# A hybrid encoder layer on one core: rotary tables moved behind the recurrence's convolutions, gate weights cleared and loaded earlier, softplus in a tile of its own

## The chip, the core and the metric

The kernel is one program on one core of a Trainium2 chip. A core has a matrix engine (PE, with its weight loads shown apart as PEld), a vector engine (DVE), an activation engine (ACT), a general engine (POOL) and a queue engine (SP) that issues DMA transfers. Each engine runs its own list of instructions in order; semaphores tie the lists together. Working tiles lie in on-chip memory (128 partitions wide), and PE writes its products into PSUM, from which DVE and ACT read.

The metric is the device time of one execution in microseconds (us), as the median of several runs. The profile is of one further execution and shows every instruction of every engine.

## The reference

One layer of a bidirectional encoder for 1024 tokens of width 1024 in f32. The part that matters here is the first of its three sub-layers, up to the attention:

```python
h = rms_norm(x, attn_norm)
proj = h @ w_in                       # 512 xr | 512 y | 256 q-latent | 128 kv-latent | 32 rope key
xf = depthwise_conv(xr, lru_conv_w[0], lru_conv_b[0], 3, 0)      # causal, width 4
xb = depthwise_conv(xr, lru_conv_w[1], lru_conv_b[1], 0, 3)      # anti-causal
hf = rg_lru(xf, w_a[0], b_a[0], w_i[0], b_i[0], lam[0], False)
hb = rg_lru(xb, w_a[1], b_a[1], w_i[1], b_i[1], lam[1], True)
lru_out = (hf + hb) * gelu(yg)

def rg_lru(x, w_a, b_a, w_i, b_i, lam, reverse):
    r = sigmoid(block_diag(x, w_a) + b_a)
    i = sigmoid(block_diag(x, w_i) + b_i)
    log_a = -8.0 * r * softplus(-lam)
    b = sqrt(-expm1(2.0 * log_a)) * (i * x)
    # h[t] = exp(log_a[t]) * h[t-1] + b[t], or from the right if reverse

def rope_tables(positions):
    inv = 10000.0 ** (-arange(0, 32, 2) / 32)
    ang = positions[..., None] * inv
    return cos(ang), sin(ang)
...
```

The tables rotate the last 32 columns of each query head and the shared rope key in the attention. Behind the attention come a cross-attention to a memory of 256 tokens and a gated feed-forward part with a width-3 convolution, which take most of the time and are not touched.

## The kernel before

The input is normalised in eight tiles of 128 tokens and transposed by PE into `hT` (L189 to L201), split into a rounded part and a remainder. Every product is made of three (`mm3`, L109): rounded by rounded, rounded by remainder, remainder by rounded. The weights are split in the same way, POOL doing the two steps (`wsplit`, L134 and L135) for all but the first.

The recurrent branch works in four units of 128 channels. For unit j, `xr_stage(j)` makes the projection (PSUM tile `psin`, two of these in turn) and both convolutions of width 4: ACT writes bias plus first tap for each direction (L348), then DVE adds three taps per direction, reading `psin` each time (L350 forward, L352 backward). `y_stage(j)` makes the gate branch's projection in the other `psin` and the gelu on ACT and DVE (L359 Square, L360, L361 Tanh, L362). `lru_stage(j)` makes for each direction the two gates (four products `psg`, L381), then the decay (Exp, L384), the input factor (Tanh L385, Sqrt L386, L388), the gated input (L389, L390 on POOL) and the scan on DVE (L393 forward, L395 backward); L397 and L399 join the directions with the gelu. A new projection can start only when the `psin` tile of the projection two before has been read for the last time: by the sixth convolution step of an `xr` unit (L352), or by the gelu's last step of a `y` unit (L362).

The stages are written in this order: xr 0, xr 1, gate weights 0, rotary tables, y 0, lru 0, xr 2, y 1, gate weights 1, lru 1, xr 3, y 2, lru 2, y 3, lru 3, then the latents (`lat_units`, `latents`, L403 on, PSUM tile `pslat` from the same pair as `psin`) and the attention. The code order is not the order on the engines: a scheduler places the instructions on each engine's list by its own estimates, and only the dependences and `tc.issue_after` bind it.

`rope_tables()` (L442) computes the sine and cosine arguments of 8 x 16 x 128 angles in a tile `rtt`: 16 one-column memsets on POOL (L445), 45 DVE instructions on 128x128 elements (L448 to L499, argument reduction in several parts), two Sin on ACT (L480, L481) and two small DMA loads of the gains (L483, L484). `rtt` has the tag "yt" with one buffer, which is also the tag of the gelu's tile `t` in `y_stage`: the tiles of the two follow one another in program order. `krs`, `rS`, `rqC` and `rqS` are its results; the first to be read is `krs`, by POOL's rotation of the shared key after the latents (`rotated`, L438 to L441).

`gate_unit(jj)` (L315) takes a tile `wgate`, clears it on POOL (L318), and loads the diagonal blocks with eight DMAs (L323).

The 15 parameter rows are loaded into the first 128 columns of a tile `RR` of six times 128 columns (L203, tag "xr", two buffers), transposed by PE and copied to `pcols`, which every bias and tap reads. The softplus of the recurrence's decay is computed from `pcols` on POOL with two steps on DVE (L277 to L296), with its temporaries `e8`, `y8`, `z8`, `w8` in `RR[:, 5]`. The convolution tiles of xr 1 have the tag "xr" as well, so that one of them has to wait until `RR` is read for the last time.

Of the kernel before, what the change touches and what calls it, by code (L numbers as in the profile page):

```python
# [11 lines left out]
F32 = mybir.dt.float32  # L12
# [3 lines left out]
ALU = mybir.AluOpType  # L16
# [3 lines left out]
S = 1024  # L20
# [63 lines left out]
def trunk_layer(ctx: ExitStack, tc: tile.TileContext, a: dict, out: bass.AP):  # L84
# [91 lines left out]
            w_first = wsplit(w_in_load(0), eng="ad")  # L176
    w_second = w_in_load(P)


    hT = [[big.tile([P, KD, 512], F32R, tag="big", name=f"hT{h}{s}") for s in range(2)] for h in range(2)]  # L180
    scr = lrup.tile([P, NJ, S], F32, tag="lru", name="scr")
# [19 lines left out]
            last_lo = dve.tensor_sub(hT[h][1][:, q * 4:q * 4 + 4, o:o + P], pv, f(hT[h][0])[:, q * 4:q * 4 + 4, o:o + P])  # L201


    RR = tp.tile([P, 6, P], F32, tag="xr", bufs=2, name="RR")
    R1, R2, R3 = RR[:, 0], RR[:, 1], RR[:, 2]
    pool.memset(R1, 0.0)
    rows = {}
# [2 lines left out]
    def addrows(name, ap, n, w=P):  # L210
        r = pos[0]
        rows[name] = r
        pos[0] += n
        nc.sync.dma_start(R1[r:r + n, :w], ap)
# [13 lines left out]
    addrows("mk_g", a["mem_k_norm"], 1)  # L228
    addrows("q_g", a["mla_q_norm"], 1, QKH)
    addrows("k_g", a["mla_k_norm"], 1, QKH)  # L230
    pcols = const.tile([P, P], F32, name="pcols")
    pt = pb1.tile([P, 512], F32, tag="b1", name="ptp")
    pe.transpose(pt[:, :P], R1, ident)
# [36 lines left out]
    pool.tensor_scalar(hb, cols("b_a", 16), 0.5, 0.0, ALU.mult, ALU.add)  # L270
    sp4 = const.tile([P, 16], F32, name="sp4")
    lam = cols("lam", 8)
    e8 = RR[:, 5, 0:8]
    y8 = RR[:, 5, 8:16]
    z8 = RR[:, 5, 16:24]
    w8 = RR[:, 5, 24:32]
    pool.tensor_scalar(z8, lam, -1.0, 0.0, ALU.mult, ALU.add)  # L277
    dve.tensor_tensor(z8, z8, lam, ALU.min)
    pool.memset(e8, math.e)
# [30 lines left out]
        return ps  # L310

    lru = lrup.tile([P, NJ, S], F32, tag="lru", name="lru")
    wg = {}

    def gate_unit(jj):  # L315

        w = wp.tile([P, 1024], F32, tag="w", name="wgate")
        pool.memset(w, 0.0)  # L318
        rv = w.rearrange("p (j d g c) -> p j d g c", j=2, d=2, g=2)
        for b in range(2):  # L320
            for gi, nm in enumerate(("lru_w_a", "lru_w_i")):
                for d in range(2):
                    nc.sync.dma_start(  # L323
                        rv[64 * b:64 * b + 64, :, d, gi, 64 * b:64 * b + 64],
                        a[nm][0, d].rearrange("(j b) p c -> b p j c", b=2)[b][:, 2 * jj:2 * jj + 2, :])
        wg[jj] = w

    ssl = const.tile([P, NT], F32, name="ssl")
    ssm = const.tile([P, NT], F32, name="ssm")
    krss = bc.tile([P, NT], F32, name="krss")  # L330
# [11 lines left out]
    def xr_stage(j):  # L342

        ps = in_proj(j * P)
        xfs = [tp.tile([P, S], F32, tag=("xf", "xr")[j % 2], bufs=2, name="xf") for _ in range(2)]
        cw = [[col("conv_w", (d * 4 + k) * 4 + j) for k in range(4)] for d in range(2)]
        for d in range(2):
            act.activation(xfs[d], ps, AF.Identity, bias=col("conv_b", d * 4 + j), scale=cw[d][3 - 3 * d])  # L348
        for n in range(1, 4):
            dve.scalar_tensor_tensor(xfs[0][:, n:], ps[:, :S - n], cw[0][3 - n], xfs[0][:, n:], ALU.mult, ALU.add)  # L350
        for n in range(1, 4):
            dve.scalar_tensor_tensor(xfs[1][:, :S - n], ps[:, n:], cw[1][n], xfs[1][:, :S - n], ALU.mult, ALU.add)  # L352
        return xfs

    def y_stage(j):
# [48 lines left out]
    def lat_units():  # L404
        for kk in range(4):
            def load(raw, kk=kk):
                nc.sync.dma_start(raw[:, :2 * LAT].rearrange("p (k c) -> p k c", k=2),
                                  w_in[kk * 2 * P:(kk + 1) * 2 * P, OFF_CQ:OFF_CQ + LAT].rearrange("(k p) c -> p k c", p=P))
            wl_.append(wunit(load, 2 * LAT))
# [31 lines left out]
    def rope_tables():  # L441
# [59 lines left out]
            rS.append(T)  # L501
        return rC, rS

    xrs = {0: xr_stage(0)}
    xrs[1] = xr_stage(1)
    gate_unit(0)
    rC, rS = rope_tables()
    y_stage(0)
    lru_stage(0, xrs[0])
    xrs[2] = xr_stage(2)  # L510
    y_stage(1)
    gate_unit(1)
    lru_stage(1, xrs[1])
    xrs[3] = xr_stage(3)
# [1 line left out]
    lru_stage(2, xrs[2])  # L516
    y_stage(3)
    lru_stage(3, xrs[3])
    lat_units()
    for t in range(NT):  # L520
        latents(t)
# [746 lines left out]
```

## Time and profile before

| | us |
|---|---|
| median of three runs | 1434.71 |
| the three runs | 1434.5, 1434.71, 1444.2 |
| the profiled execution, own time | 1439.12 |
| its span in the profile | 1437.0 |

The profiled execution lasted 2.1 us longer than the span that its profile shows, and 4.4 us longer than the median. A row of the timeline gives start, duration, engine, line, operation, output and inputs, the shapes, a count, and in brackets how long the engine had been idle before it and what released it. A row with a count above 1 puts neighbouring instructions of one form together, with the sum of their time. A row of the windows view gives, for a stretch of time, its length and the busy time of each engine (with the count of instructions), then the clock granted to PE (1.00 is full), the share of the DMA engines and the rate.

### The profile page before, as it was taken

How to read it: one execution, taken by the hardware profiler on the slowest of the kernel's cores; microseconds unless marked ns; L12 is line 12 of the kernel's file. 1: busy time of each engine (PE TensorE's matmuls, PEld its weight loads, DVE VectorE, ACT ScalarE, POOL GpSimd, SP SyncE). 2: the span in 40 equal slices, each digit the busy share in tenths (PEclk: the TensorE clock that was granted, in tenths of full speed). 3: DMA queues.
4: the chain of work that ended last, by engine and by line, in shares of the span. 5: the costliest groups of instructions: out<-in, count | busy, mean ns of one | idle time of the engine just before them, and what ended most of it. 6: DMA issues, size and time to landing. Idle time of an engine off the chain costs nothing.

```text
span 1437.0 us, 18317 instructions
## 1 busy us (share of the span) xinstructions
PE 1377.6 (96%) x6832; PEld 1153.7 (80%) x6832; DVE 903.6 (63%) x1236; ACT 603.0 (42%) x955; POOL 579.3 (40%) x597
## 2 busy tenths in 40 slices
PE   6898899998999999999999999999999999999998
PEld 5666698787889888888887888888888888888887
DVE  6787747899998856576644665443443445665553
ACT  5374945688888842355422111111111122433331
POOL 6653544557696811021239999322332310000000
PEclk9899999999999999999999999999999999999999
DMA  5301101200000052101008888322223222666763
GB/s 197 84 14 42 61 16 45 74 1 1 1 1 1 14 170 81 46 14 30 30 17 285 288 292 275 125 80 89 96 92 99 96 74 96 198 213 206 222 195 103
DMA packets 114231, 145.94 MB, mean 102 GB/s; under 512 B 9546, under 2 KB 64095, under 8 KB 114143
## 3 DMA queue, kind: packets, MB, share of 16 engines
q1 hardware_dynamic: 114143, 144.78, 31.0%
q8 instruction: 54, 0.88, 0.3%
q14 instruction: 34, 0.28, 0.1%
HBM read 105.95 MB, written 38.80 MB: 101 GB/s over the span
## 4 chain that ended last, share of the span: by engine, by line
PE 77%; DVE 9%; ACT 7%; POOL 2%; issue 2%; DMA 1%; SPq 0%; ACTq 0%; DVEq 0%; POOLq 0%
PE psup L109 33%; PE psdn L109 8%; PE psdw L109 6%; PE psP L109 6%; PE psq L109 3%; PE psS L109 3%; PE psmo L109 3%; PE po L109 3%; PE psin L109 2%; PE pslat L109 2%; PE psT L767 2%; DVE st L748 2%; DVE pT L771 2%; PE pq L109 1%; PE pkv L109 1%
## 5 line engine op out<-in xcount | busy, mean ns | idle before, releaser
L109 PE MATMUL psup<-h,whi 128*128 128x512 f32 x1408 | 434.4, 389 | 1.1 <-DVE gu L1158 0.9
L109 PEld LDWEIGHTS psup<-h,whi 128*128 128x128 f32 x1408 | 264.2, 188 | 56.6 <-POOL ws L1182 1.2
L109 PE MATMUL psup<-h,wlo 128*128 128x512 f32 x704 | 273.9, 389 | 0.0
L1157 DVE SCALAR_TENSOR_TENSOR gu<-psup,fcw,gu 128x1023 f32<-128x1023 f32 x44 | 56.4, 1281 | 187.6 <-ACT gu L1156 183.0
L1156 ACT ACTIVATE gu<-psup,fcw 128x1024 f32<-128x1024 f32 x44 | 53.3, 1211 | 287.2 <-PE psup L109 287.2
L1215 DVE TENSOR_TENSOR dlo<-rawd,dhi 128x1024 fp32r<-128x1024 f32 x77 | 93.5, 1223 | 101.0 <-ACT dhi L1214 101.0
L109 PEld LDWEIGHTS psup<-h,wlo 128*128 128x128 f32 x704 | 132.2, 188 | 27.4
L1214 ACT ACTIVATE dhi<-rawd 128x1024 fp32r<-128x1024 f32 x77 | 81.5, 1061 | 158.7 <-PE psdn L109 51.0
L134 POOL TENSOR_SCALAR whi<-raw 128x1024 fp32r<-128x1024 f32 (+2 forms) x58 | 70.2, 1210 | 192.0 <-PE psup L109 176.6
L135 POOL TENSOR_TENSOR wlo<-raw,whi 128x1024 fp32r<-128x1024 f32 (+2 forms) x58 | 143.8, 2479 | 9.1 <-PE psin L109 5.7
L109 PE MATMUL psS<-kT,qT 96*128 96x512 f32 x384 | 103.8, 404 | 3.9 <-ACT pr L752 3.8
L109 PE MATMUL psin<-hT,whi 128*128 128x512 f32 (+1 forms) x288 | 88.2, 390 | 7.9 <-DVE xf L352 6.6
L754 POOL TENSOR_SCALAR pr<-pr,st 128x1024 f32<-128x1024 f32 x64 | 72.0, 1125 | 54.1 <-DVE st L753 32.2
L771 DVE TENSOR_TENSOR pT<-psT,pT 128x512 fp32r<-128x512 f32 x128 | 84.4, 678 | 5.9 <-ACT pT L770 5.8
L752 ACT ACTIVATE pr<-psS,st,rqk 128x1024 f32<-128x1024 f32 x64 | 77.2, 1207 | 17.8 <-DVE st L750 13.3
L748 DVE TENSOR_REDUCE st<-psS 128x1 f32<-128x1024 f32 x64 | 77.7, 1214 | 8.1 <-PE psS L109 7.8
L109 PEld LDWEIGHTS psS<-kT,qT 96*128 96x128 f32 x384 | 67.6, 189 | 17.6 <-ACT pr L752 6.2
L1182 POOL TENSOR_TENSOR ws<-rawd 128x512 f32<-128x512 f32 x55 | 81.4, 1508 | 0.0
L109 PE MATMUL po<-pT,vt 128*128 128x256 f32 x512 | 72.3, 287 | 3.9 <-DVE pT L771 3.7
L770 ACT ACTIVATE pT<-psT 128x512 fp32r<-128x512 f32 x128 | 70.9, 596 | 8.1 <-PE psT L767 7.6
L767 PE MATMUL psT<-ident,pr 128*128 128x128 f32 x512 | 68.3, 273 | 5.7 <-POOL pr L754 3.7
L109 PEld LDWEIGHTS psin<-hT,whi 128*128 128x128 f32 x288 | 54.7, 198 | 21.1 <-issue 9.6
(303 smaller groups left out, 2832.5 us busy)
## 6 DMA issues: line engine op xcount, KB each, us to landing
raw<-in_w_up SPq DMA_DIRECT2D x44, 512.0 KB
rawd<-ad SPq DMA_DIRECT2D x77, 256.0 KB
wd<-ws SPq DMA_DIRECT2D x55, 256.0 KB
ad<-as SPq DMA_DIRECT2D x55, 256.0 KB
rawd<-wd SPq DMA_DIRECT2D x55, 256.0 KB
rawd<-in_w_down SPq DMA_DIRECT2D x22, 512.0 KB
ad<-gu SPq DMA_DIRECT2D x22, 256.0 KB
rawd<-in_w_down SPq DMA_DIRECT2D x22, 256.0 KB
```

The lines of the kernel that those rows point to most:

```text
L109: return pe.matmul(ps, lhsT=l, rhs=r, start=start, stop=stop)
L134: pool.tensor_scalar(hi[:, sl], raw[:, sl], 1.0, 0.0, ALU.mult, ALU.add)
L135: pool.tensor_sub(lo[:, sl], raw[:, sl], f(hi)[:, sl])
L748: dve.tensor_reduce(st[:, 0:1], psS, AX.X, ALU.max, negate=True)
L752: act.activation(pr, psS, AF.Exp, bias=st[:, 1:2], scale=r, accum_out=st[:, 2:3])
L754: scaled[s] = pool.tensor_scalar(pr, pr, st[:, 3:4], 0.0, ALU.mult, ALU.add)
L767: pe.transpose(ps[:, i * P:(i + 1) * P], pr[:, (n * 4 + i) * P:(n * 4 + i + 1) * P], ident)
L770: act.activation(dh, pv, AF.Copy)
L771: dve.tensor_sub(pTs[s // 2][n][1][:, :, qi * P:(qi + 1) * P], pv, f(dh))
L1182: pool.tensor_tensor(st, raws[h0][:, c0], raws[h1][:, c1], op)
L1214: act.activation(hi, raw, AF.Copy)
L1215: dve.tensor_sub(lo, raw, f(hi))
```

## The change

Three things change in the source.

The call of `rope_tables()` goes from between `xr_stage(1)` and `y_stage(0)` to behind `lru_stage(3)`, with the condition that none of its instructions is issued ahead of the last backward convolution step of the last unit (`last_conv[-1]`). Since `rtt` shares the buffer "yt", its 16 memsets now wait for the gelu of `y_stage(3)`.

`gate_unit` is split: `gate_zero(jj)` clears the tile, `gate_unit(jj)` loads it. For the first two units of the recurrence the clearing is placed ahead of the input's normalisation, and the loading right behind the parameter rows. For the other two both stand where `gate_unit(1)` stood.

`RR` loses its sixth row, and softplus's temporaries get a small tile `spc` of their own, so that softplus no longer keeps a convolution tile of xr 1 waiting.

```diff
+    def gate_zero(jj):
+        wg[jj] = wp.tile([P, 1024], F32, tag="w", name="wgate")
+        pool.memset(wg[jj], 0.0)
+    def gate_unit(jj):
+        rv = wg[jj].rearrange("p (j d g c) -> p j d g c", j=2, d=2, g=2)
...
+    gate_zero(0)
...
-    RR = tp.tile([P, 6, P], F32, tag="xr", bufs=2, name="RR")
+    RR = tp.tile([P, 5, P], F32, tag="xr", bufs=2, name="RR")
...
     addrows("k_g", a["mla_k_norm"], 1, QKH)
+    gate_unit(0)
...
-    e8 = RR[:, 5, 0:8]
-    y8 = RR[:, 5, 8:16]
-    z8 = RR[:, 5, 16:24]
-    w8 = RR[:, 5, 24:32]
+    spc = sm.tile([P, 4, 8], F32, tag="spc", bufs=1, name="spc")
+    e8, y8, z8, w8 = spc[:, 0], spc[:, 1], spc[:, 2], spc[:, 3]
...
-            dve.scalar_tensor_tensor(xfs[1][:, :S - n], ps[:, n:], cw[1][n], xfs[1][:, :S - n], ALU.mult, ALU.add)
+            last_conv.append(dve.scalar_tensor_tensor(xfs[1][:, :S - n], ps[:, n:], cw[1][n], xfs[1][:, :S - n],
+                                                      ALU.mult, ALU.add))
...
+    last_conv = []
     xrs = {0: xr_stage(0)}
     xrs[1] = xr_stage(1)
-    gate_unit(0)
-    rC, rS = rope_tables()
     y_stage(0)
     lru_stage(0, xrs[0])
     xrs[2] = xr_stage(2)
     y_stage(1)
+    gate_zero(1)
     gate_unit(1)
...
     lru_stage(3, xrs[3])
+    with tc.issue_after(last_conv[-1].ins):
+        rC, rS = rope_tables()
     lat_units()
```

The scheduler makes another order of this on every engine up to the attention; behind that the orders are the same. Most line numbers of the kernel after are larger by 2 to 5 from `gate_unit`'s old place on (convolution L352 and L354, gelu L362 to L365, recurrence L384 to L402, tables L451 to L502), and by 17 or 18 ahead of it.

On DVE, this is what stood around the first convolutions before (the numbers in the names tell buffers apart; `xf_463` and `xf_464` are the two directions of unit 0):

```order
L282 RECIPROCAL RR_285<-RR_285 128x8
L459 SCALAR_TENSOR_TENSOR rtt_546<-rtt_546 128x128
L350 SCALAR_TENSOR_TENSOR xf_463<-psin_366,pcols_302,xf_463 128x1023
L459 SCALAR_TENSOR_TENSOR rtt_546<-rtt_546 128x128
L350 SCALAR_TENSOR_TENSOR xf_463<-psin_366,pcols_302,xf_463 128x1022
L453 TENSOR_SCALAR rtt_546<-rtt_546 128x128
L470 TENSOR_TENSOR rtt_546<-rtt_546 128x128
L350 SCALAR_TENSOR_TENSOR xf_463<-psin_366,pcols_302,xf_463 128x1021
L352 SCALAR_TENSOR_TENSOR xf_464<-psin_366,pcols_302,xf_464 128x1023
```

And this is DVE's list at the same place in the kernel after (`xf_474` and `xf_475` are unit 0, `xf_537` the forward direction of unit 1):

```order
L295 TENSOR_TENSOR spc_337<-spc_337,pcols_312 128x8
L352 SCALAR_TENSOR_TENSOR xf_474<-psin_377,pcols_312,xf_474 128x1023
L352 SCALAR_TENSOR_TENSOR xf_474<-psin_377,pcols_312,xf_474 128x1022
L352 SCALAR_TENSOR_TENSOR xf_474<-psin_377,pcols_312,xf_474 128x1021
L354 SCALAR_TENSOR_TENSOR xf_475<-psin_377,pcols_312,xf_475 128x1023
L299 RECIPROCAL spc_337<-spc_337 128x8
L354 SCALAR_TENSOR_TENSOR xf_475<-psin_377,pcols_312,xf_475 128x1022
L352 SCALAR_TENSOR_TENSOR xf_537<-psin_488,pcols_312,xf_537 128x1023
L354 SCALAR_TENSOR_TENSOR xf_475<-psin_377,pcols_312,xf_475 128x1021
```

The table steps are gone from here, softplus's reciprocal stands between two steps of the backward convolution, and one step of unit 1 stands ahead of unit 0's sixth.

In the middle of the recurrence the convolutions of unit 3 stood on DVE as follows before (`xf_955` is unit 3's forward direction, `thi_863` and `thi_885` the two directions of unit 1, whose forward scan L393 stood ahead of all convolutions of unit 2):

```order
L360 SCALAR_TENSOR_TENSOR yt_839<-yt_839,psin_790 128x1024
L362 SCALAR_TENSOR_TENSOR lru_358<-yt_839,psin_790 128x1024
L389 SCALAR_TENSOR_TENSOR thi_885<-thi_885,xf_527 128x1024
L388 SCALAR_TENSOR_TENSOR thr_884<-av_890,thr_884 128x1024
L395 SCALAR_TENSOR_TENSOR thi_885<-av_890,thi_885 128x1024
L397 TENSOR_TENSOR thi_863<-thi_863,thi_885 128x1024
L399 SCALAR_TENSOR_TENSOR lru_358<-thi_863,lru_358 128x1024
L350 SCALAR_TENSOR_TENSOR xf_955<-psin_906,pcols_302,xf_955 128x1023
```

The same stretch of DVE's list after (`xf_889` is unit 3's forward direction, `thi_797` and `thi_819` the two directions of unit 1):

```order
L363 SCALAR_TENSOR_TENSOR yt_773<-yt_773,psin_724 128x1024
L365 SCALAR_TENSOR_TENSOR lru_369<-yt_773,psin_724 128x1024
L392 SCALAR_TENSOR_TENSOR thi_797<-thi_797,xf_537 128x1024
L391 SCALAR_TENSOR_TENSOR thr_796<-av_802,thr_796 128x1024
L396 SCALAR_TENSOR_TENSOR thi_797<-av_802,thi_797 128x1024
L392 SCALAR_TENSOR_TENSOR thi_819<-thi_819,xf_538 128x1024
L391 SCALAR_TENSOR_TENSOR thr_818<-av_824,thr_818 128x1024
L398 SCALAR_TENSOR_TENSOR thi_819<-av_824,thi_819 128x1024
L352 SCALAR_TENSOR_TENSOR xf_889<-psin_840,pcols_312,xf_889 128x1023
L400 TENSOR_TENSOR thi_797<-thi_797,thi_819 128x1024
L352 SCALAR_TENSOR_TENSOR xf_889<-psin_840,pcols_312,xf_889 128x1022
```

Both directions of unit 1 now stand between the gelu of `y_stage(1)` and unit 3's convolutions, and the joins L400 and L402 stand between the convolution's steps.

At the end of the recurrence, where before only the steps of unit 3 stood (L397 and L399 of unit 2, then L388, L390 and L393 of unit 3), DVE's list after reads (`thi_1074` is unit 3's forward direction):

```order
L365 SCALAR_TENSOR_TENSOR lru_369<-yt_1060,psin_1011 128x1024
L400 TENSOR_TENSOR thi_968<-thi_968,thi_990 128x1024
L392 SCALAR_TENSOR_TENSOR thi_1074<-thi_1074,xf_889 128x1024
L451 TENSOR_TENSOR rtt_1111<-posc_332,rtt_1111 128x128
L402 SCALAR_TENSOR_TENSOR lru_369<-thi_968,lru_369 128x1024
L456 TENSOR_SCALAR rtt_1111<-rtt_1111 128x128
L457 TENSOR_SCALAR rtt_1111<-rtt_1111 128x128
L391 SCALAR_TENSOR_TENSOR thr_1073<-av_1079,thr_1073 128x1024
L466 SCALAR_TENSOR_TENSOR rtt_1111<-rtt_1111 128x128
L456 TENSOR_SCALAR rtt_1111<-rtt_1111 128x128
L393 TENSOR_TENSOR thi_1074<-thi_1074,thr_1073 128x1024
```

Five of the 45 table steps (L451, L456, L457, L466, L456) now stand ahead of unit 3's product L393; the others follow it, among the scans and the latents' scalings.

On SP's queue these loads stood behind the parameter rows before (rows of the same form are counted):

```order
L214 DMA RR<-in_mla_k_norm 1x96
L249 DMA RR<-in_ffn_conv_w 88x128
L250 DMA RR<-in_ffn_conv_w 44x128
L251 DMA RR<-in_ffn_conv_b 44x128
L260 DMA RR<-in_positions 8x128
L483 DMA rtt<-in_mla_q_norm 128x32
L484 DMA rtt<-in_mla_k_norm 128x32
L155 DMA raw<-in_w_in 128x8x128 x2
L323 DMA wgate<-in_lru_w_a 64x2x64 x2
L323 DMA wgate<-in_lru_w_i 64x2x64 x2
```

After, the same place of SP's queue has:

```order
L232 DMA RR<-in_mla_k_norm 1x96
L191 DMA wgate<-in_lru_w_a 64x2x64 x2
L191 DMA wgate<-in_lru_w_i 64x2x64 x2
L191 DMA wgate<-in_lru_w_a 64x2x64 x2
L191 DMA wgate<-in_lru_w_i 64x2x64 x2
L268 DMA RR<-in_ffn_conv_w 88x128
L269 DMA RR<-in_ffn_conv_w 44x128
L270 DMA RR<-in_ffn_conv_b 44x128
L279 DMA RR<-in_positions 8x128
L155 DMA raw<-in_w_in 128x8x128 x5
```

The eight gate loads come ahead of the third input weight block and of the positions, and the two gain loads of `rtt` have left; they stand now behind the load of `w_ukv` and ahead of those of `w_mem_kv`.

More of the change, by code (lines that the diff above doesn't have):

```diff
@@ L177, in trunk_layer @@
     w_second = w_in_load(P)
+    wg = {}
+    def gate_zero(jj):
[3 more added lines that the diff above has]
+        rv = wg[jj].rearrange("p (j d g c) -> p j d g c", j=2, d=2, g=2)
+        for b in range(2):
+            for gi, nm in enumerate(("lru_w_a", "lru_w_i")):
+                for d in range(2):
+                    nc.sync.dma_start(
+                        rv[64 * b:64 * b + 64, :, d, gi, 64 * b:64 * b + 64],
+                        a[nm][0, d].rearrange("(j b) p c -> b p j c", b=2)[b][:, 2 * jj:2 * jj + 2, :])
+    gate_zero(0)
     hT = [[big.tile([P, KD, 512], F32R, tag="big", name=f"hT{h}{s}") for s in range(2)] for h in range(2)]
@@ L312, in trunk_layer @@
     lru = lrup.tile([P, NJ, S], F32, tag="lru", name="lru")
[L313 to L326, printed above, removed]
     ssl = const.tile([P, NT], F32, name="ssl")
```

## The prediction

> **What bounds the kernel now.** I read the busy shares first, then PE's idle stretches up to the attention in the windows view, then the timeline of the engine that ends each of them.
>
> ```profile
> PE 1377.6 (96%) x6832; PEld 1153.7 (80%) x6832; DVE 903.6 (63%) x1236; ACT 603.0 (42%) x955; POOL 579.3 (40%) x597
> core 0: us, PE busy (x) PEld busy (x) DVE busy (x) ACT busy (x) POOL busy (x), PEclk, DMA share, GB/s
> 33.90:38.40 4.50, 4.50 (x17) 3.72 (x18) 3.05 (x5) 1.08 (x2) 4.33 (x4) 0.62 0.55 147
> 50.50:56.70 6.20, 0.08 (x1) 0.00 (x0) 6.20 (x10) 1.20 (x1) 5.70 (x9) 0.90 0.48 124
> 56.70:62.60 5.90, 5.86 (x8) 2.53 (x9) 4.37 (x7) 1.73 (x3) 4.53 (x17) 0.52 0.56 158
> 109.80:115.00 5.20, 0.09 (x1) 0.00 (x0) 5.10 (x5) 0.30 (x1) 1.11 (x2) 0.86 0.28 82
> 115.00:120.00 5.00, 4.92 (x12) 3.89 (x13) 3.44 (x3) 3.87 (x5) 0.00 (x0) 0.50 0.00 0
> 139.60:173.30 33.70, 33.70 (x128) 23.70 (x126) 23.32 (x17) 33.39 (x37) 16.34 (x10) 1.00 0.19 59
> 185.00:211.00 26.00, 26.00 (x146) 25.47 (x145) 8.20 (x15) 8.43 (x29) 7.50 (x12) 1.00 0.00 1
> 42.60:71.50 28.90, 16.14 (x45) 0.62 (x2) 0.00 (x0) 0.88 0.28 75
> ```
>
> The last row counts the tile `rtt` alone; its engines are DVE, ACT and POOL. PE works 96% of the span, so the whole gain lies in a few waits. DVE is busy in all of 50.5 to 56.7 and nearly all of 109.8 to 115.0 while PE stands still, and PE runs at half clock behind each. From 139.6 to 173.3 ACT is busy for 33.39 of 33.70 us: there ACT is the bound, and PE's time means little. From 185 on PE is never idle, so what arrives there is carried to the end.
>
> **First gate and first gelu projection.** These rows end PE's first wait:
>
> ```profile
> 44.93 2.31 ACT L348 ACTIVATE xf<-psin,pcols 128x1024 f32<-128x1024 f32 x2 [9.29 <-DVE rtt L459]
> 46.37 2.45 POOL L135 TENSOR_TENSOR wlo<-raw,whi 128x1024 fp32r<-128x1024 f32 x1
> 46.61 3.20 DVE L454 TENSOR_SCALAR rtt<-rtt 128x128 f32<-128x128 f32 x1
> 50.20 0.39 PE L109 MATMUL psin<-hT,wlo 128*128 128x512 f32 x1
> 50.80 0.19 DVE L282 RECIPROCAL RR<-RR 128x8 f32<-128x8 f32 x1
> 55.26 1.27 DVE L350 SCALAR_TENSOR_TENSOR xf<-psin,pcols,xf 128x1021 f32<-128x1021 f32 x1
> 56.74 6.44 PE L109 MATMUL psg<-xf,wgate 128*128 128x512 f32 x8 [6.16 <-issue]
> 59.31 1.27 DVE L352 SCALAR_TENSOR_TENSOR xf<-psin,pcols,xf 128x1021 f32<-128x1021 f32 x1
> 62.62 1.02 PE L109 MATMUL psin<-hT,whi 128*128 128x512 f32 x2
> 62.84 0.20 POOL L296 TENSOR_SCALAR sp<-sp 128x8 f32<-128x8 f32 x1
> 73.94 3.59 PE L109 MATMUL psg<-xf,wgate 128*128 128x512 f32 x8
> ```
>
> The gate at 56.74 starts right behind the third forward step (55.26 + 1.27 = 56.53). The forward direction's bias was there at 44.93 + 1.16 = 46.1, so without the table steps its three convolution steps (1.27 each) end at 49.9. PE finishes the second projection at 50.20 + 0.39 = 50.6. The gate then follows at 50.6, 6.1 earlier, without the idle time. The y 0 projection needs the sixth step: by the new order seven convolution steps and a reciprocal stand ahead on DVE, 46.1 + 7 x 1.27 + 0.2 = 55.2, against 62.62: -7.4. PE is free from 54.2 by the warm gate duration (3.59 instead of 6.44 for 8 rows), so PE waits only about 1 us there.
>
> **To the end of y 1.**
>
> ```profile
> 70.97 1.24 ACT L384 ACTIVATE av<-thr,sp 128x1024 f32<-128x1024 f32 x1
> 75.95 2.58 DVE L388 SCALAR_TENSOR_TENSOR thr<-av,thr 128x1024 f32<-128x1024 f32 x1 [0.79 <-ACT thr L386]
> 84.43 0.70 PE L109 MATMUL psin<-hT,whi 128*128 128x512 f32 x2 [1.42 <-DVE xf L352]
> 106.50 1.02 ACT L359 ACTIVATE yt<-psin 128x1024 f32<-128x1024 f32 x1 [8.57 <-PE psin L109]
> ```
>
> A projection takes 73.94 - 62.62 = 11.3, or (106.50 - 84.43) / 2 = 11.0. Between y 0 and xr 2 PE had two sets of gates and 1.4 + 1.4 us of waits; now one set stands there, the second goes behind y 1. So 55.2 + 11.3 + 3.6 + 22.1 = 92.2, against 106.50: -14.3. Softplus was ready at 62.84 + 0.20 = 63.0 and no table step delays it now; with the Exp not ahead of 63.0 and 75.95 - 70.97 = 5.0 from Exp to Sqrt, ACT is through at 68, behind which y 0's Square comes. That is 1.4 after y 0's end (66.5), hidden under the gates and xr 2.
>
> **Unit 3's projection and y 2.**
>
> ```profile
> 88.05 1.23 DVE L388 SCALAR_TENSOR_TENSOR thr<-av,thr 128x1024 f32<-128x1024 f32 x1 [0.46 <-ACT thr L386]
> 89.36 2.40 POOL L390 TENSOR_TENSOR thi<-thi,thr 128x1024 f32<-128x1024 f32 x1 [8.38 <-DVE thr L388]
> 98.29 3.24 DVE L397 TENSOR_TENSOR thi<-thi 128x1024 f32<-128x1024 f32 x1
> 115.08 1.19 PE L109 MATMUL psin<-hT,whi 128*128 128x512 f32 x2 [5.19 <-DVE xf L352]
> 126.85 2.29 DVE L395 TENSOR_TENSOR_SCAN thi<-av,thi 128x1024 f32<-128x1024 f32 x1 [2.51 <-POOL thi L390]
> 139.60 1.02 ACT L359 ACTIVATE yt<-psin 128x1024 f32<-128x1024 f32 x1 [8.58 <-PE psin L109]
> 149.03 1.06 ACT L386 ACTIVATE thr<-thr 128x1024 f32<-128x1024 f32 x1
> ```
>
> Unit 3's projection waits for unit 2's sixth convolution step, which stands behind both directions of unit 0 and their joins. From y 0's Square at 68 to the next Sqrt's end ACT takes 149.03 + 1.06 - 139.60 = 10.5: 78.5. Then L388 1.23, the product 2.40 and the scan 2.29 give 84.4; the two joins 1.2 to 3.2 each and six steps 7.6 give 94.4 to 98.4. I take 96.4, the middle, since PE is free at 95.8 anyway (92.2 + 3.6): -18.7 against 115.08. From there to y 2's end it was 139.60 - 115.08 = 24.5. The half-clock stretch (4.92 us of work at 0.50, 2.5 us lost) does not come without a wait of PE, and one set of gates more lies inside: 24.5 - 2.5 + 3.6 = 25.6, so 122.0: -17.6.
>
> **y 3, where a new wait opens.** Now both directions of unit 1 stand on DVE ahead of unit 3's convolutions, and y 3 needs the sixth of these.
>
> ```profile
> 142.43 1.03 PE L109 MATMUL psin<-hT,whi 128*128 128x512 f32 x2
> 157.54 1.06 ACT L386 ACTIVATE thr<-thr 128x1024 f32<-128x1024 f32 x1
> 158.50 1.01 ACT L359 ACTIVATE yt<-psin 128x1024 f32<-128x1024 f32 x1
> 179.12 0.71 PE L109 MATMUL pslat<-whi,hT 128*128 128x416 f32 x1 [5.77 <-ACT pslat L426]
> ```
>
> From y 1's end at 92.2 the forward direction takes 10.5, the backward one 157.54 + 1.06 - 150.09 = 8.5, then 5.9 to the scan's end as above and six steps with two joins 10 to 14: 127.1 to 131.1. I take 129 (middle; the joins ran beside POOL's work once in 3.24). Against 142.43: -13.4. PE is done with its gates at 122.0 + 3.6 = 125.6, so it idles some 3 us here. Then 11.3 + 3.6 to y 3's end, and half of the 2.5 us of a half-clock stretch because the idle time lies between those that cooled PE (5.19 and 6.16) and none: 145.2, -13.3 against 158.50.
>
> ```profile
> 33.89 1.06 PE L198 MATMUL psx<-ident,xt 128*128 128x128 f32 x8 [2.15 <-DVE xt L192]
> ```
>
> This row shows a mean clock of 0.62 (window 33.9 to 38.4) after an idle time of 2.15 us only. [...]
>
> **The tail and the tables there.** ACT has the same list from 158.50 to the third latent tile at 179.12, 20.6 us, so the shift would pass whole. But 45 table steps (16.14 us busy, 0.36 each) now lie on DVE between, five of them ahead of unit 3's product. Cheapest they cost 5 x 0.36 = 1.8; if one waits behind a POOL step of 2.40, 4.2. I take 2.4, nearer the lower end, because one such step in 45 took 3.20. So -13.3 + 2.4 = -10.9 at the third latent tile, and by the unbroken PE after 185, to the end. The tables have time:
>
> ```profile
> 212.18 0.78 POOL L438 TENSOR_TENSOR krs<-cns,krs 128x256 f32<-128x256 f32 x1
> ```
>
> They start behind y 3's gelu at about 149, took 28.9 before, end at 178 to 187 and are first read at 212.18 - 10.9 = 201. If that cover is gone, POOL's key rotation and with it the attention wait.
>
> **Gate weights and softplus tile.**
>
> ```profile
> 23.30 0.38 SPq L155 DMA_DIRECT2D raw<-in_w_in  x1
> 33.22 1.37 SPq L323 DMA_DIRECT2D wgate<-in_lru_w_a  x2
> ```
>
> The eight gate loads at 0.68 each (5.5 us) come ahead of the third weight block and two gain loads (0.8) leave: it is issued at about 28 instead of 23.30. POOL starts its split when it is free at about 32; a landing later than that pushes POOL by 0 to 2. The memset gone from POOL's queue there gives back up to 1. Gate weights were issued by 38.5 before and first used at 56.74, so loading them earlier gains nothing. I count 0 and keep +2 for the range. The softplus tile frees a convolution buffer of unit 1; its gain is already in the order above. The gain loads stand on SP ahead of `w_mem_kv` and wait for y 3's gelu at 149; they are waited for by no load that PE needs before 185.
>
> **Sum.** 1437.0 - 10.9 = 1426.1 of span; with 2.1 around it that execution would take 1428.2. It stood 4.4 above the median, so 1434.7 - 10.9 = 1423.8, say 1424.
>
> **Rivals.**
> 1. Swallowed in the tail, 0.19. y 3 starts at the late end (131.1, +2.1), the half clock is whole (+1.3), the tables cost 4.2 (+1.8) and POOL is pushed (+2): about 1431. For it speaks that L454 took 3.20 us beside POOL's split of 46.37, and L397 3.24, and that POOL is busy for 16.34 of 33.70 us in the stretch to which the tables go; against it that the 44 other table steps averaged 0.29 (16.14 - 3.20 over 44) beside POOL's other splits.
> 2. No new wait at y 3, 0.18. The joins run in 1.2 and the ACT chain finishes earlier than counted, so PE goes on at 125.6, at full clock: 125.6 + 14.9 = 140.5, -18.0, and with the tables 2.4: 1434.7 - 15.6 = 1419. Against it stands the ACT chain of 10.5 + 8.5, the densest rows here.
> 3. Slower, 0.03: the tables aren't ready for the key rotation. It decides once they take longer than 201 - 149 = 52 us instead of 28.9. If all 45 waited for a POOL step, 45 x (0.36 + 2.40) = 124, 72 late: 1434.7 - 10.9 + 72 = 1496. More than 1% slower needs 25 + 52 = 77 us of tables, 1.7 each. Against it: the mean was 0.36 beside POOL's splits. [...]
> That the early gate weights do nothing lies inside the forecast.
>
> **Chances.** Forecast 0.60 (own range 1421 to 1428), rivals 0.19, 0.18 and 0.03. The range 1416 to 1433 takes in rivals 1 and 2 but for their outer ends. A measurement can tell about 1% of this kernel from no change, 14.3 us: below 1420.4 lie rival 2 and a little of the forecast, 0.20; above 1449 rival 3, 0.03; the rest, 0.77, is within.
>
> **What would show it.** In the changed profile: first psg at about 50.6 without idle time; y 0's psin at 55; unit 3's psin at 96 and no half clock behind it; an idle time of about 3 us ahead of y 3's psin at 129; the third latent tile at 168; table steps on DVE from 149 on and key rotation not waiting for `krs`. Wrong if y 3 starts before 126 or after 133, or if a wait on POOL's rotation appears.

## The result and the profile after

| | before | after |
|---|---|---|
| median of 19 runs, us | 1436.04 | 1428.32 |
| lowest and highest, us | 1433.52 to 1444.33 | 1426.33 to 1435.98 |
| the profiled execution, own time, us | 1439.12 | 1427.24 |
| its span, us | 1437.0 | 1425.2 |

The ratio of after to before is 0.9947, with a 95% interval of 0.9933 to 0.9961: by the median of before the kernel after is 5.6 to 9.6 us faster, within the 1% that counted as no change. Its median lies in the range given (1416 to 1433), 4.3 us above the point and 0.3 us above the forecast's own range (1421 to 1428). The two profiled executions are 11.9 us apart, more than the medians; the experiments show why.

The page of the kernel after gives the busy time of each engine:

```profile
PE 1372.9 (96%) x6832; PEld 1151.4 (81%) x6832; DVE 894.0 (63%) x1236; ACT 601.6 (42%) x954; POOL 577.0 (40%) x597
```

PE's busy time fell by 4.7 us (1377.6 before) with the same 6832 products; the windows show less half-clock time, and the mean granted clock is 0.994 against 0.990. They give, for the kernel after, the length of a stretch, the busy time of PE, PEld, DVE, ACT and POOL, the granted clock, the share of the DMA engines and the rate:

```profile
33.10:38.00 4.90, 4.80 (x26) 4.13 (x27) 3.19 (x5) 1.09 (x2) 4.62 (x4) 1.00 0.45 120
42.00:48.90 6.90, 6.28 (x30) 4.94 (x29) 4.03 (x5) 2.82 (x3) 6.59 (x8) 1.00 0.55 152
125.60:131.10 5.50, 0.02 (x1) 0.02 (x1) 5.43 (x6) 0.00 (x0) 1.95 (x2) 0.79 0.26 72
131.10:136.00 4.90, 4.89 (x12) 3.85 (x13) 3.29 (x3) 3.87 (x5) 0.00 (x0) 0.54 0.00 0
185.00:201.00 16.00, 16.00 (x90) 15.30 (x88) 5.05 (x19) 7.83 (x25) 7.18 (x10) 1.00 0.02 5
```

The same view of the tile `rtt` alone, for DVE, ACT and POOL:

```profile
155.00:190.00 35.00, 13.11 (x45) 0.62 (x2) 0.60 (x16) 0.90 0.07 22
```

The half clock at 34 to 38 is gone (1.00 over 33.1 to 38.0, against 0.62), and so are the idle time at 50.5 and the half clock behind it; PE works nearly without a pause until the first gate. A new idle time stands at 125.6 to 131.1, where DVE is busy for 5.43 of 5.50 us, with a half clock behind it. From 185 to 201 PE is busy all the time, as it was before from 185 to 211. The 45 table steps took 13.1 us where they stand now, less than the 16.1 before.

The timeline of PE and ACT in the kernel after, at the starts that the prediction named:

```profile
33.20 1.07 PE L216 MATMUL psx<-ident,xt 128*128 128x128 f32 x8 [1.26 <-DVE xt L210]
48.98 3.24 PE L109 MATMUL psg<-xf,wgate 128*128 128x512 f32 x7 [0.70 <-issue]
53.92 0.70 PE L109 MATMUL psin<-hT,whi 128*128 128x512 f32 x2 [1.26 <-DVE xf L354]
90.33 1.02 ACT L362 ACTIVATE yt<-psin 128x1024 f32<-128x1024 f32 x1 [8.57 <-PE psin L109]
95.79 0.70 PE L109 MATMUL psin<-hT,whi 128*128 128x512 f32 x2 [2.06 <-DVE xf L354]
96.80 1.06 ACT L364 ACTIVATE yt<-yt 128x1024 f32<-128x1024 f32 x1 [2.87 <-DVE yt L363]
121.37 1.02 ACT L362 ACTIVATE yt<-psin 128x1024 f32<-128x1024 f32 x1 [6.86 <-PE psin L109]
131.11 1.19 PE L109 MATMUL psin<-hT,whi 128*128 128x512 f32 x2 [5.49 <-DVE xf L354]
132.13 1.06 ACT L364 ACTIVATE yt<-yt 128x1024 f32<-128x1024 f32 x1 [6.58 <-DVE yt L363]
147.00 1.02 ACT L362 ACTIVATE yt<-psin 128x1024 f32<-128x1024 f32 x1
167.65 0.71 PE L109 MATMUL pslat<-whi,hT 128*128 128x416 f32 x1 [4.74 <-ACT pslat L429]
```

The first gate (48.98) comes 7.8 us earlier than before, y 0's projection 8.7, y 1's Square 16.2, unit 3's projection 19.3, y 2's Square 18.2. Then a part is lost: y 3's projection starts 5.49 us after PE was free, only 11.3 earlier than before. y 3's Square and the third latent tile come 11.5 us earlier, and that is what reaches the end of this execution.

What held y 3 up is on DVE. Its timeline in the kernel after:

```profile
87.90 3.91 DVE L352 SCALAR_TENSOR_TENSOR xf<-psin,pcols,xf 128x1023 f32<-128x1023 f32 x3
91.73 3.91 DVE L354 SCALAR_TENSOR_TENSOR xf<-psin,pcols,xf 128x1023 f32<-128x1023 f32 x3
95.55 1.21 DVE L363 SCALAR_TENSOR_TENSOR yt<-yt,psin 128x1024 f32<-128x1024 f32 x1
...
116.09 4.05 DVE L398 TENSOR_TENSOR_SCAN thi<-av,thi 128x1024 f32<-128x1024 f32 x1 [2.52 <-POOL thi L393]
120.06 1.25 DVE L352 SCALAR_TENSOR_TENSOR xf<-psin,pcols,xf 128x1023 f32<-128x1023 f32 x1
121.24 1.81 DVE L400 TENSOR_TENSOR thi<-thi 128x1024 f32<-128x1024 f32 x1
122.97 1.27 DVE L352 SCALAR_TENSOR_TENSOR xf<-psin,pcols,xf 128x1022 f32<-128x1022 f32 x1
124.17 1.78 DVE L402 SCALAR_TENSOR_TENSOR lru<-thi,lru 128x1024 f32<-128x1024 f32 x1
125.87 1.27 DVE L352 SCALAR_TENSOR_TENSOR xf<-psin,pcols,xf 128x1021 f32<-128x1021 f32 x1
127.06 3.90 DVE L354 SCALAR_TENSOR_TENSOR xf<-psin,pcols,xf 128x1023 f32<-128x1023 f32 x3
130.88 1.21 DVE L363 SCALAR_TENSOR_TENSOR yt<-yt,psin 128x1024 f32<-128x1024 f32 x1
```

Unit 3's convolution (L352, L354) starts at 120.06, behind unit 1's backward scan (L398), and the two joins (L400, L402) stand between its steps: 4.05 + 1.81 + 1.78 us. ACT shows two waits of the same kind: y 1's tanh (96.80) waited 2.87 us for L363, which stood behind unit 2's six convolution steps (87.90 to 95.55), and y 2's tanh (132.13) waited 6.58 us for L363 at 130.88. The tables end in time; the last step that writes `krs` and the rotation that first reads it are these, on DVE and POOL:

```profile
188.91 0.28 DVE L500 TENSOR_TENSOR krs<-rtt 128x128 f32<-128x128 f32 x1
200.44 0.78 POOL L441 TENSOR_TENSOR krs<-cns,krs 128x256 f32<-128x256 f32 x1
```

### The profile page after: what moved, and what is told of

It reads as the page before. It is cut to its first block, busy times and chain, and to the rows that moved or that the text cites. A ratio compares the mean times of both kernels' runs of the same rounds, so it can differ in the third digit from the quotient of the medians.

```text
span 1425.2 us, 18313 instructions
## 1 busy us (share of the span) xinstructions
PE 1372.9 (96%) x6832; PEld 1151.4 (81%) x6832; DVE 894.0 (63%) x1236; ACT 601.6 (42%) x954; POOL 577.0 (40%) x597
## 4 chain that ended last, share of the span: by engine, by line
PE 76%; DVE 9%; ACT 5%; POOL 4%; issue 4%; DMA 1%; SPq 0%; POOLq 0%; ACTq 0%; DVEq 0%
PE psup L109 33%; PE psdn L109 8%; PE psdw L109 6%; PE psP L109 6%; PE psq L109 3%; PE psS L109 3%; PE po L109 3%; PE psmo L109 3%; PE psin L109 2%; DVE st L753 2%; PE psT L772 2%; DVE pT L776 2%; PE pslat L109 1%; PE pq L109 1%; ACT pr L757 1%
## 5 line engine op out<-in xcount | busy, mean ns | idle before, releaser
L135 POOL TENSOR_TENSOR wlo<-raw,whi 128x1024 fp32r<-128x1024 f32 (+2 forms) x58 | 146.9, 2534 | 3.2
L109 PE MATMUL psS<-kT,qT 96*128 96x512 f32 x384 | 103.8, 404 | 3.9 <-ACT pr L757 3.8
```

The costliest lines, as they stand in the source:

```text
L109: return pe.matmul(ps, lhsT=l, rhs=r, start=start, stop=stop)
L135: pool.tensor_sub(lo[:, sl], raw[:, sl], f(hi)[:, sl])
```

## The experiments

The kernels below were compared with the kernel before on the same chip; a ratio is that of the kernel to before.

### The tables moved alone

```diff
-    rC, rS = rope_tables()
     y_stage(0)
...
     lru_stage(3, xrs[3])
+    with tc.issue_after(last_conv[-1].ins):
+        rC, rS = rope_tables()
```

> The kernel before with the rotary tables moved behind the last convolution, and nothing else. Theory A (the move of the tables carries the whole gain, the other two parts add nothing that lasts): first gate at about 50 us instead of 56.7, gelu projection y 0 at 51 to 55 instead of 62.6, y 3's projection at 127 to 132, third latent tile at 167 to 169; the time 6 to 10 us below before. Theory B (the parts need one another, because softplus's row in RR still holds a convolution tile of unit 1): unit 1's convolutions and the projections xr 2 and xr 3 come some 8 us later than in the kernel after, and no more than 3 us of the gain is left.

Measured: 1430.43 us against 1438.24, ratio 0.9946 (0.9924 to 0.9968). First gate at 49.75, y 0's projection at 53.51, y 3's at 134.18. Later rows of its timeline are these, of PE and ACT:

```profile
70.61 5.40 PE L109 MATMUL psg<-xf,wgate 128*128 128x512 f32 x8 [2.52 <-ACT thr L382]
150.24 1.01 ACT L360 ACTIVATE yt<-psin 128x1024 f32<-128x1024 f32 x1
170.86 0.71 PE L109 MATMUL pslat<-whi,hT 128*128 128x416 f32 x1 [5.78 <-ACT pslat L427]
```

Theory B, which left no more than 3 us, falls. By the medians theory A holds: this one edit has as good a ratio as the whole change, 0.9947. The trace is less clear. y 3's projection comes later than the 127 to 132 that A named, and the third latent tile later than its 167 to 169, 3.2 us behind the whole change. The fastest executions agree with the trace: 1429.58 against 1433.60 here, 4.0 us, and 1426.33 against 1433.52 for the whole change, 7.2 us. So the tables carry more than half of the gain; whether the other two parts add nothing or some 3 us is open.

### The gate weights alone

```diff
+    gate_zero(0)
...
     addrows("k_g", a["mla_k_norm"], 1, QKH)
+    gate_unit(0)
...
-    gate_unit(0)
     rC, rS = rope_tables()
```

> The kernel before with the first gate weights cleared early and loaded right behind the parameter rows, and nothing else. Theory A: nothing to gain, since the first gate waits for the convolution; the third weight block is issued some 5 us later and lands about when POOL gets to it: between 0 and 3 us slower than before. Theory B: a few us faster, because POOL's clear and eight DMA issues leave the busy stretch.

Measured: 1442.17 against 1438.24, ratio 1.0025 (1.0000 to 1.0051): no gain, and probably a loss of some us. Theory B falls, and the 3.9 us lie above the 0 to 3 of theory A. The first gate came at 57.49 behind 9.35 us of idle time. On DVE the table steps stood ahead of the convolution as before, and two steps of one form (L457, the L453 of the kernel before) show in this kernel's timeline as

```profile
45.48 3.38 DVE L457 TENSOR_SCALAR rtt<-rtt 128x128 f32<-128x128 f32 x2
```

where the first such pair took 0.36 us in the kernel before. That the scheduler's other order sets them beside more of POOL's work is the author's estimate from this row; it was not shown. The late weight block that theory A named is there as well: POOL's split at 35.71 waited 3.35 us for it (0.36 in the kernel after). But PE ended its second projection at 48.1 all the same, earlier than before (50.6), so this is not what held the first gate.

### Softplus's tile alone

```diff
-    RR = tp.tile([P, 6, P], F32, tag="xr", bufs=2, name="RR")
+    RR = tp.tile([P, 5, P], F32, tag="xr", bufs=2, name="RR")
...
-    e8 = RR[:, 5, 0:8]
...
+    spc = sm.tile([P, 4, 8], F32, tag="spc", bufs=1, name="spc")
+    e8, y8, z8, w8 = spc[:, 0], spc[:, 1], spc[:, 2], spc[:, 3]
```

> The kernel before with softplus's temporaries in a tile of their own, and nothing else. Theory A: unit 1's convolutions and xr 3's projection start some us earlier (xr 3 at 105 to 112 instead of 115), but y 3 waits for unit 3's convolutions behind unit 1's scans and gives it back: within 3 us of before. Theory B: a lasting gain of 4 us or more, with y 3 earlier by as much as xr 3.

Measured: 1440.21 against 1438.24, ratio 1.0016 (0.9998 to 1.0034). Two starts on PE in this kernel's timeline, unit 3's projection and y 3's:

```profile
106.24 1.19 PE L109 MATMUL psin<-hT,whi 128*128 128x512 f32 x2 [5.03 <-DVE xf L350]
142.34 1.19 PE L109 MATMUL psin<-hT,whi 128*128 128x512 f32 x2 [3.83 <-DVE xf L350]
```

Unit 3's projection comes 8.8 us earlier than before (115.08), y 3's at the same time as before (142.43), behind a wait that was not there. What the tile frees is given back at y 3, as theory A said. One thing is unlike in these two profiles: the one shown of before has a half clock at 34 to 38 us, and this one has not (1.00 there). The third profile of before, in the last of these sections, has none either. Against that one unit 3's projection is 4.6 us earlier (110.84 there), y 3's 4.7 us later (137.68) and the third latent tile 4.4 us later (178.79 against 174.43), so in this pair more is lost than was won. In the medians the 2 us are not clear of the noise.

### The whole change without one part

Without the early gate weights:

```diff
-    gate_zero(0)
...
     addrows("k_g", a["mla_k_norm"], 1, QKH)
-    gate_unit(0)
...
     xrs[1] = xr_stage(1)
+    gate_unit(0)
```

(`gate_unit` clears its tile itself again.)

> The kernel after without the early gate weights (clear and loads where they were before). Theory A: nothing waits for the gate weights in either, so the time is that of the kernel after within 2 us. Theory D (the 3.9 us that the early loads cost when made alone lie in the whole change too, behind the later third weight block): 3 to 4 us below the kernel after.

Measured: 1428.87, ratio 0.9940 (0.9918 to 0.9962), against 1427.91 of the kernel after on the same chip. Theory A holds; theory D, which wanted 3 to 4 us less than the kernel after, is not borne out. The third latent tile comes at 168.99, 1.3 us later than in the kernel after: the early weights gained a little there instead of costing. This profiled execution had the half clock at 34 to 38 us (0.64 and 0.51 in the windows 34 to 36 and 36 to 38), which the kernel after has not (1.00 in both). So with the tables gone from the first convolutions that half clock costs about 1.3 us at the third latent tile, if the early weights do nothing else; two profiles of the kernel before, one with it and one without, differ by 4.7 us there (last section).

Without softplus's tile:

```diff
-    RR = tp.tile([P, 5, P], F32, tag="xr", bufs=2, name="RR")
+    RR = tp.tile([P, 6, P], F32, tag="xr", bufs=2, name="RR")
...
-    spc = sm.tile([P, 4, 8], F32, tag="spc", bufs=1, name="spc")
-    e8, y8, z8, w8 = spc[:, 0], spc[:, 1], spc[:, 2], spc[:, 3]
+    e8 = RR[:, 5, 0:8]
...
```

> The kernel after without the tile for softplus (its temporaries stay in RR's sixth row). Theory A: xr 2 and xr 3 come 6 to 8 us later than in the kernel after, because RR holds one of unit 1's convolution tiles, but y 3 finds no scans ahead of unit 3's convolutions and starts without a wait at 129 to 132; y 3's Square at 147 to 150, and the time within 3 us of the kernel after (the replayed order says 1 us slower). Theory B (the softplus tile carries part of the gain): 4 us or more slower than the kernel after.

Measured: 1430.50, ratio 0.9961 (0.9942 to 0.9980). Unit 3's projection came at 106.88 (95.79 in the kernel after), y 3's without a wait at 133.76 (131.11), its Square at 149.83 (147.00) and the third latent tile at 170.45 (167.65). Of the 11.1 us that the tile saves at unit 3's projection, 2.8 reach the third latent tile. The mechanism is that of theory A, though unit 3's projection is later than its 6 to 8 us and y 3's later than its 129 to 132. The time does not decide between A and B: it lies 2.6 us above the kernel after, which ran on another chip, and 3.9 us above the kernel with the early clear below, which ran on the same one, and the intervals of the ratios overlap.

### The kernel after once more, and without the tables

> The kernel after once more, on the chip of the three kernels below, as their measure: 7 to 10 us below before, with the same waits as in its first profile (y 3's projection at about 131 behind 5.5 us of idle time).

Measured: 1427.91 against 1438.89, ratio 0.9930 (0.9907 to 0.9953), and the same waits (y 3's projection at 131.29 behind 5.66 us). The gain of 11.0 us is a little more than expected.

The profiled execution lasted 1432.96 us, 5.7 more than the first one of this kernel, and it reaches the third latent tile at the same time (167.76). What it loses, it loses in the attention. One small step on DVE there is, in the first profile of the kernel after,

```profile
407.45 1.15 DVE L565 TENSOR_SCALAR rqk<-rqk 128x8 f32<-128x8 f32 x1
```

and in this one, with the product on PE that follows:

```profile
407.02 4.62 DVE L565 TENSOR_SCALAR rqk<-rqk 128x8 f32<-128x8 f32 x1
413.51 2.26 PE L109 MATMUL po<-pT,vt 128*128 128x256 f32 x9 [4.37 <-DVE pT L776]
```

From 410 to 420 us PE is busy for 6.49 of 10.00 us at a mean clock of 0.66 (9.53 at 1.00 in the first profile). The profiled execution without softplus's tile (1435.91 us) has the same long step (4.60 us) and the same wait (4.34 us), with a clock of 0.74 from 410 to 420. Executions of the kernel after thus come in more than one kind too.

For the next run the diff is

```diff
+    rST = sm.tile([P, NT, ROPE], F32, tag="rS", bufs=1, name="rS")
+    rC, rS = [rqC, krs], [rqS, rST]
+    for T, v in ((rqC, 1.0), (krs, 1.0), (rqS, 0.0), (rST, 0.0)):
+        pool.memset(T, v)
...
-    with tc.issue_after(last_conv[-1].ins):
-        rC, rS = rope_tables()
```

> The kernel after with the rotary tables left out: their four tiles are set to one and zero at the start, so queries and keys are not rotated, and the 45 vector steps, two Sin and two gain loads are gone. It prices the tables where they stand now. By the prediction's term: 2.4 us below the kernel after (1.8 to 4.2). By the kernel after's profile (ACT from y 3's Square to the third latent tile 20.65 us, against 20.62 before): less than 1 us.

Measured: 1428.01, ratio 0.9936 (0.9912 to 0.9959), beside 1427.91 with the tables. From y 3's Square to the third latent tile it took 20.62 us, with the tables 20.65:

```profile
147.53 1.01 ACT L362 ACTIVATE yt<-psin 128x1024 f32<-128x1024 f32 x1
168.15 0.71 PE L109 MATMUL pslat<-whi,hT 128*128 128x416 f32 x1 [4.72 <-ACT pslat L429]
```

Where they stand now the tables cost nothing that can be seen: the term of 2.4 us is not there.

### The scans held behind the convolutions

`lru_stage` gets an argument; with it, the backward scan and the joins become a function of their own (`join`), which is called behind the convolutions of the unit two further on.

```diff
-            else:
+            elif not hold:
                 dve.tensor_tensor_scan(h[:, ::-1], av[:, ::-1], thi[:, ::-1], 0.0, ALU.mult, ALU.add)
...
-    lru_stage(0, xrs[0])
+    join0 = lru_stage(0, xrs[0], hold=True)
     xrs[2] = xr_stage(2)
+    with tc.issue_after(last_conv[-1].ins):
+        join0()
...
-    lru_stage(1, xrs[1])
+    join1 = lru_stage(1, xrs[1], hold=True)
     xrs[3] = xr_stage(3)
+    with tc.issue_after(last_conv[-1].ins):
+        join1()
```

> The kernel after, with the backward scans and the joins of units 0 and 1 held behind the convolutions of units 2 and 3. Theory A (y 3's wait in the kernel after is made on DVE by unit 1's backward scan and two joins, 4.05 + 1.81 + 1.78 us ahead of and among unit 3's convolutions): y 3's projection starts right behind unit 2's gates at 119 to 125, without idle time and half clock, y 3's Square at 136 to 141 instead of 147, and the time is 5 to 8 us below the kernel after. Theory C (ACT is the bound there, PE's wait only shows it): the wait moves to ACT's gelu and gate steps, y 3's Square stays at 145 or later, and no more than 2 us are won.

Measured: 1420.84, ratio 0.9882 (0.9857 to 0.9907), 7.1 us below the kernel after on the same chip. The windows view of this kernel from y 2's end on:

```profile
118.70:126.00 7.30, 7.30 (x25) 4.52 (x24) 7.30 (x6) 7.01 (x9) 6.23 (x3) 1.00 0.20 54
```

Its timeline of DVE, ACT and PE:

```profile
111.44 3.92 DVE L352 SCALAR_TENSOR_TENSOR xf<-psin,pcols,xf 128x1023 f32<-128x1023 f32 x3 [0.96 <-ACT xf L350]
115.27 3.91 DVE L354 SCALAR_TENSOR_TENSOR xf<-psin,pcols,xf 128x1023 f32<-128x1023 f32 x3
119.09 2.28 DVE L403 TENSOR_TENSOR_SCAN thi<-av,thi 128x1024 f32<-128x1024 f32 x1
...
137.93 1.00 ACT L362 ACTIVATE yt<-psin 128x1024 f32<-128x1024 f32 x1
158.54 0.71 PE L109 MATMUL pslat<-whi,hT 128*128 128x416 f32 x1 [5.87 <-ACT pslat L436]
```

Unit 3's convolutions run from 111.44 to 119.2, the scan (now L403) behind them, PE goes from y 2 over unit 2's gates to y 3 (121.76) without idle time and at a clock of 1.00, and y 3's Square comes at 137.93. Theory A holds and theory C falls: ACT's waits went with PE's. The hold of unit 0 has a part in this. With it unit 2's convolution ended at 89.4 (95.6 in the kernel after), y 1's tanh did not wait, and ACT's forward direction took 10.5 us (90.22 to 100.70) instead of 13.5. What the hold of each unit is worth by itself was not tried.

### The early clear without the early loads, and with the held scans

```diff
     addrows("k_g", a["mla_k_norm"], 1, QKH)
-    gate_unit(0)
...
     y_stage(0)
+    gate_unit(0)
```

> The kernel after with the first gate weights cleared early but loaded behind the third weight block, as before. In the kernel after, DVE's last two normalising steps take 3.53 us instead of 4.42, PE waits 1.26 instead of 2.15 us for them and does not fall to half clock at 34 to 38 us, and the second projection ends 1.6 us earlier. Theory M (POOL's clear at 32.2 held up the DVE step beside it): the same here, first gate at about 49. Theory N (POOL stands still for the third weight block, which is late behind the eight gate loads, and this gap lets DVE through): POOL goes straight on to its split here, the two steps take 4.4 again, PE waits 2.1 us, and the first gate comes at 50 to 51.

Measured: 1426.62, ratio 0.9936 (0.9912 to 0.9960). DVE's last two normalising steps and POOL's instructions beside the second, in the timeline of the kernel before:

```profile
29.32 4.42 DVE L192 TENSOR_SCALAR xt<-xt,rs 128x1024 f32<-128x1024 f32 x2 [2.52 <-POOL rs L146]
29.78 2.52 POOL L135 TENSOR_TENSOR wlo<-raw,whi 128x1024 fp32r<-128x1024 f32 x1
32.24 0.95 POOL L318 MEMSET wgate<- 128x1024 f32 x1
```

And in the timeline of this kernel:

```profile
29.40 3.54 DVE L210 TENSOR_SCALAR xt<-xt,rs 128x1024 f32<-128x1024 f32 x2 [2.55 <-POOL rs L146]
29.85 2.54 POOL L135 TENSOR_TENSOR wlo<-raw,whi 128x1024 fp32r<-128x1024 f32 x1
32.36 1.48 POOL L134 TENSOR_SCALAR whi<-raw 128x1024 fp32r<-128x1024 f32 x1
```

The two steps take 3.54 us although POOL goes straight on; this time it is POOL's split step that takes 1.48 us, where the next one of that form takes 1.05. PE waits 1.25 us, keeps its clock (1.00 from 34 to 38), and the first gate comes at 48.87. That is theory M: the clear had held the vector step up. The place of the eight loads matters little: with them early the first gate came at 48.98. The greater part of this wait stays: of the two vector steps the first takes 0.75 us in both kernels and the second 3.60 us before and 2.71 us here. In both it ends 0.55 us behind the end of a POOL instruction: of the clear before (33.19), of L135 here (32.39).

Both edits together:

> Held scans and late gate loads together (the clear stays early). If both readings hold (y 3's wait was unit 1's scan and joins on DVE; the early clear alone keeps PE from half clock at 34 us, and the place of the loads is worth at most 1 us), no half clock ahead of the third latent tile, that tile at 157.5 to 159, and the time 16 to 20 us below before, within 2 us of the held scans. If the held scans' lead over the kernel after was chance, it lies at 1426 to 1429.

Measured: 1419.10, ratio 0.9861 (0.9829 to 0.9893); the third latent tile at 160.02, 1 us later than expected, and no half clock (1.00 in every window of 2 us up to 156) until the wait of 6.82 us in front of it. Its median is the lowest here, 8.8 us below that of the kernel after once more. Its 1.7 us below the held scans alone are not clear of the noise: the lowest run of both is 1417.38.

### The kernel before, twice more

> The kernel before once more, for a second profile of it. The first one lasted 1439.1 us, 4 us above most of its runs, and had the clock at a half in five stretches. If that is why its span lay 11.8 us above the span after while the medians differ by 7.7, then an execution of about 1434 us lacks one or two of these stretches, and the places of the waits are the same.

> The kernel before a third time. Its executions lie between 1433.6 and 1445 us with mean clocks of 0.993 to 0.987, and both profiles so far had 0.990 and five half-clock stretches. If this one lies near 1434, it shows which stretch or wait such an execution lacks; near 1439 it should repeat the two.

Measured: 1439.03 and 1433.24 us. The first repeats the profile shown of before: first gate at 56.78, half clock at 34 to 38 (0.72 and 0.50 in its two windows), third latent tile at 179.02. The second has the idle time of PE ahead of the last transposes as well (2.15 us), but no half clock behind it. From its windows view:

```profile
33.90:38.40 4.50, 4.50 (x24) 3.87 (x25) 3.04 (x5) 1.09 (x2) 4.33 (x4) 1.00 0.55 147
```

And from its timeline of PE:

```profile
33.87 1.06 PE L198 MATMUL psx<-ident,xt 128*128 128x128 f32 x8 [2.15 <-DVE xt L192]
53.60 3.63 PE L109 MATMUL psg<-xf,wgate 128*128 128x512 f32 x4 [4.64 <-POOL whi L134]
174.43 0.71 PE L109 MATMUL pslat<-whi,hT 128*128 128x416 f32 x1 [5.84 <-ACT pslat L426]
```

The second projection ends 1.6 us earlier than in the first profile (48.96 against 50.59), the first gate comes 3.1 us earlier and the third latent tile 4.7 us. Executions of the kernel before are thus of at least two kinds, with and without this half clock, and the difference grows on its way, first through the table steps.

## Why the prediction was right, and where its sum was off

The direction, the range and the mechanism stand. Point by point:

- **First gate and y 0.** Forecast 50.6 and 55.2, measured 48.98 and 53.92. DVE's list was read rightly; the 1.6 us more come from the second projection, which ended at 48.28 instead of 50.6 because PE waited 0.9 us less at 33 us (1.26 against 2.15) and kept its clock there (1.00 against 0.62). The gate still waited 0.70 us for the convolution, which began only when both of ACT's bias steps were done (42.63 + 2.30 = 44.93); the prediction counted on one. The prediction counted the early clear as 0 to 1 us on POOL and did not see that it stood beside the vector step for which PE waits. The run with the early clear and the late loads shows it.
- **To the end of y 1 and unit 3's projection.** Forecast 92.2 and 96.4, measured 90.33 and 95.79; y 2's Square 122.0 against 121.37. These terms hold.
- **The new wait at y 3.** Named in advance with its cause, and too small: 3 us of idle time and half of a half-clock loss were forecast, 5.49 us and the whole stretch (clock 0.54 over 4.9 us) measured. The start at 131.11 is the late end of 127.1 to 131.1. From y 1's end to there it took 40.8 us instead of 36.8. Two terms were short. ACT's forward direction took 13.5 us from Square to Sqrt's end (90.33 to 103.8) instead of 10.5, because L363 stood behind six convolution steps, a wait that DVE's list showed and the prediction left out. And the scan took 4.05 instead of 2.29. The held scans show that DVE's order makes this wait and the first of the two terms: with another order ACT takes 10.5 us again, y 3 does not wait, and the end comes 7 us earlier.
- **The tail.** Forecast 2.4 us for the tables, measured nothing: ACT took 20.65 us from y 3's Square to the third latent tile (20.62 before), and without the tables the time was the same.
- **The third latent tile.** Forecast 10.9 us earlier, measured 11.5 between the profiles: too little at the first gate and too much in the tail stood against too little at y 3. That these errors nearly cancel is luck. The way from there to the end is not PE without a pause, as the prediction had it: from 200 to 400 us PE was busy for 187.4 of 200 us before and 187.3 after. In these two executions the shift passed whole even so (1257.9 us from there to the span's end before, 1257.6 after); in the second profile of the kernel after it did not (1263.1).
- **From the profile to the median.** Here is the step that failed in size: the 10.9 were taken from the median as a whole, with the words that the profiled execution "stood 4.4 above the median". These 4.4 us were no even offset. By the third profile they were for the most part the half clock at 34 us and what it did to the stretch behind (4.7 of the 5.7 us between the two spans), which this change removes; an execution without it (1433.24 us, third latent tile at 174.43) has only 174.43 - 167.65 = 6.8 us to lose. The fastest runs of the two kernels are 7.2 us apart. The medians mix executions of several kinds and fell by 7.7. The base was off as well: 1434.7 was the median of three runs, and that of 19 is 1436.04, so 1.3 of the 4.3 us above the point come from there.
- **The rivals.** The first was right that y 3 would start at the late end and at half clock, and wrong that the tables cost 4.2 us; the measured time lies between its 1431 and the forecast. The second needed y 3 to start at 125.6; no kernel but those with held scans did so. The third did not come near: the tables ended at 189.2, 11 us ahead of the rotation at 200.44, though their steps began at 158.0 and not at 149, behind y 3's last gelu step, which ended on DVE at 155.8.

## What to carry to other kernels

When work is taken from in front of a wait, ask which instructions come to stand in front of the next one: 19.3 us were won at unit 3's projection, and 8 of these were lost, mostly to scans and joins that the new list put ahead of a convolution. What PE's next stage needs goes ahead of what only has to be done at some time.

A profile is one execution. If PE's clock falls in some executions and not in others (0.62 and 1.00 over 33.9 to 38.4 in two of the kernel before), the gain against the profile is not the gain against the median; take a second and a third profile of before, and of after.

## What was not expected of the hardware

An idle time of 2.13 to 2.15 us in front of the last transposes was followed by half clock in two profiles of the kernel before and by full clock in the third (window 33.9 to 38.4: 0.62 in the first and 1.00 in the third; windows 34 to 36 and 36 to 38: 0.72 and 0.50 in the second). Of the three other kernels with 2.15 us there one fell (0.64 and 0.51 in these two windows, without the early gate weights) and two did not (1.00, with the tables moved alone and with softplus's tile alone). After 1.25 or 1.26 us none of the eight profiles of kernels with the early clear fell (1.00 in both windows). In the kernel with the tables moved alone the clock fell at an idle time of 2.52 us between gate products (70.61 above; 0.75 and 0.50 in the windows 70 to 72 and 72 to 74). Around the pause of 2.15 us PE made only transposes, in the first profile of the kernel before (30.70 to 34.95) as in the third (30.69 to 34.93); what decides between the two outcomes no run here shows.

A clear of 0.95 us on POOL beside a vector step held that step up by 0.9 us (4.42 against 3.54 for two, without the clear there). In that kernel POOL's split step beside the vector step took 0.43 us longer than the next one (1.48 against 1.05). In both kernels the vector step ended 0.55 us behind the end of a POOL instruction. Whether one of the two engines waits for the other there is not shown: no run varied the order by itself. Whether the long step in the attention (4.62 us instead of 1.15) is of the same kind was not tried.
